# Low parts of the streamed weights of an attention stage, tied on VectorE to the scaling of the scores last written

## The chip, the cores and the metric

The kernel runs on one core of a Trainium2 chip. The metric is the time of one execution on the device in microseconds. Three timed runs of the kernel before the change took 1510.47 to 1513.23 us, with a median of 1512.52 us. One execution more was recorded by the profiler.

## The reference

One encoder layer works on 512 tokens of width 1024. One projection gives all inputs of two attentions of eight heads each: a neighbourhood attention in two dimensions and a latent attention with low-rank queries and keys. Their outputs, side by side, go through one output projection, a residual sum and a LayerNorm, and then through a layer of experts that is most of the time of the kernel and that this change does not touch.

```python
z = h @ W_in        # NA q | NA k | NA v | MLA c_q | MLA c_kv | MLA k_rope
a_na  = neighbourhood attention (8 heads, window 8 x 16, 2-D relative bias)
a_mla = latent attention (8 heads, low-rank q / kv, rotary key)
h = LN1(alpha * h + concat(a_na, a_mla) @ W_o)
h = LN2(alpha * h + PEER(h) + sigmoid(h @ W_g + b_g) * (p @ W_ple))
```

## The kernel before, in words

All products of weights and activations are made from split operands. `split` (L101 to L112) makes of a float32 tile a high part by a cast on ScalarE, and a low part, the difference of the tile and its high part, by a subtraction on VectorE. `mm3` (L122 to L125) then makes three matmuls: high by high, low by high, high by low. A weight is loaded by `stream` (L114): it takes one of three buffers `raw`, issues a DMA from SyncE, and splits into `whi` and `wlo`, of which there are two each. A buffer `raw` is free for the next load when both parts have been made of it.

The attention works in units, one for each head (or pair's half) and block of 128 query rows. Units 0 to 31 are those of the neighbourhood attention, in the first half of the stage, units 32 to 63 those of the latent attention. A unit has four steps: three matmuls give scores in PSUM; VectorE takes the maximum (L607 for the neighbourhood heads together with the bias, L718 for the latent ones) and negates it (L209), ScalarE takes the exponential with the sum (L210), VectorE the reciprocal (L211) and the scaling (L212), all but the maximum in `soft`; TensorE transposes the scaled scores (L219) and ScalarE copies them out (L221); TensorE multiplies them with the values (L622, L732). `run_heads` emits the scores of a unit two units ahead of its transposes, and in between the steps of the next heads' projections (`feeds`).

`next_weight` (L487) hands a projection its weight and at once prefetches the following one, so a weight has one projection's time to arrive and be split. The order of its users on TensorE is query, key and so on, as in `srcs`. `load_w2` (L737 to L742) loads the second half of the output weight w_o in four quarters and splits them into `w2h` and `w2l`, in one step of a feed; they are read only at the end of the output projection.

What sets the order: on TensorE the order is the one in which the code is written (`manual_schedule` with that engine alone). On VectorE, ScalarE, SyncE and GpSimd a scheduler of the framework orders the instructions, by its own model of costs, under the dependencies that it knows. A caller can add a dependency that orders two instructions on an engine without a semaphore: `split` does it for every entry of the list `turned`, which holds one instruction for the cast and one for the subtraction. In the stage of the change the list is empty before.

Of the kernel before, what the change touches and what calls it, by code (L numbers as in the profile page):

```python
# [15 lines left out]
OP = mybir.AluOpType  # L16
# [57 lines left out]
def tile_encoder_layer(ctx: ExitStack, tc: tile.TileContext, A: dict, out: bass.AP):  # L74
    nc = tc.nc
# [20 lines left out]
    def r32(ap):  # L96
        return ap.bitcast(F32)

    turned = []

    def split(hi, lo, src, scale=None):  # L101

        if scale is None:
            cut = nc.scalar.copy(hi, src), nc.vector.tensor_tensor(lo, src, r32(hi), op=OP.subtract)  # L104
            for ins, prev in zip(cut, turned):
                tc.add_manual_dep(ins.ins, prev.ins.name, mybir.DependencyInfo(mybir.DependencyClass.NoSync,
                                                                               mybir.DependencyReason.DATA),
                                  reason="order")
            return cut
        else:  # L110
            nc.scalar.mul(hi, src, scale)
            nc.vector.scalar_tensor_tensor(lo, src, scale, r32(hi), op0=OP.mult, op1=OP.subtract)  # L112

    def stream(src, shape, scale=None):  # L114
        raw = wst.tile([128] + shape, F32, name="raw", bufs=3)
        nc.sync.dma_start(raw, src)
        hi = wst.tile([128] + shape, F32R, name="whi")
        lo = wst.tile([128] + shape, F32R, name="wlo")
        cut = split(hi, lo, raw, scale)
        return (hi, lo, cut[0]) if cut else (hi, lo)  # L120
# [73 lines left out]
    def transpose_to(dst_h, dst_l, src, c):  # L194

        for g in range(2):
            ps = ps_tile("tr")
            for i in range(4):
                d = 4 * g + i
                nc.tensor.transpose(ps[:, i * 128:(i + 1) * 128], src[:, d * 128:(d + 1) * 128], ident)  # L200
            v = ps.rearrange("p (a b) -> p a b", b=128)
            cut = split(dst_h[:, 4 * g:4 * g + 4, c * 128:(c + 1) * 128],
                        dst_l[:, 4 * g:4 * g + 4, c * 128:(c + 1) * 128], v)
        return cut

    def soft(s_in, p, nk, mx, scale=1.0, minus=-1.0):

        mx, nmx, sm, rs = (mx[:, i:i + 1] for i in range(4))
        nc.vector.tensor_scalar(nmx, mx, minus, None, op0=OP.mult)  # L209
        nc.scalar.activation(p[:, :nk], s_in, AF.Exp, bias=nmx, scale=scale, accum_out=sm)  # L210
        nc.vector.reciprocal(rs, sm)  # L211
        nc.vector.tensor_scalar(p[:, :nk], p[:, :nk], rs, None, op0=OP.mult)  # L212

    def transposed(p, nk):
        ps = ps_tile("tr")
# [62 lines left out]
    with tc.tile_pool(name="ln0", bufs=1, reuse_waits="tile") as ln0, \  # L278
# [126 lines left out]
        for x in parts:  # L405
            split(*x)
# [80 lines left out]
    def next_weight():  # L487
        w = ready.pop() if ready else stream(*srcs.pop(0))
        if srcs:
            ready.append(stream(*srcs.pop(0)))  # L490
        return w

    def latent_k(i, lat):
# [44 lines left out]
    def latent_q(i):  # L538
        w = next_weight()
        ps = ps_tile("pj")  # L540
        yield from proj_steps(ps, w)
        split(cqh[:, i], cql[:, i], ps, gq[:, i:i + 1])
        if i == 0:
            nc.scalar.activation(sq_q, ps, AF.Square)
        else:
            sq = aw.tile([128, T], F32, name="p_exp", bufs=4)
            nc.scalar.activation(sq, ps, AF.Square)
            nc.vector.tensor_tensor(sq_q, sq_q, sq, op=OP.add)
# [12 lines left out]
    def rope_key():  # L561
        w = next_weight()
        ps = ps_tile("pj")
        yield from proj_steps(ps[:64], w, 64)
        kt = aw.tile([128, T], F32, name="p_exp", bufs=4)[:32]
        kt2 = aw.tile([128, T], F32, name="p_exp", bufs=4)[:32]
        nc.vector.tensor_tensor(kt, ps[0:32], cosT[0:32], op=OP.mult)
        nc.vector.tensor_tensor(kt2, ps[32:64], sinT[32:64], op=OP.mult)
        nc.vector.tensor_tensor(kt, kt, kt2, op=OP.add)
        split(krh, krl, kt)  # L570
# [10 lines left out]
    def na_proj(m):  # L581
        w = next_weight()
        ps = ps_tile("pj")
        yield from proj_steps(ps, w)
        qh, ql = na_q[m % 2]
        for hh in range(2):
            rows = slice(64 * hh, 64 * hh + 64)
            split(qh[rows, hh], ql[rows, hh], ps[rows], 0.125)
        w = next_weight()
        ps = ps_tile("pj")  # L590
        yield from proj_steps(ps, w)
        kh = ip.tile([128, T], F32R, name="na_kh")
        kl = ip.tile([128, T], F32R, name="na_kl")
        split(kh, kl, ps)
        na_k[m] = (kh, kl)

    def na_scores(m, b, hh):
        (qh, ql), (kh, kl) = na_q[m % 2], na_k[m]
        bias = ip.tile([128, NA_KEYS], F32, name="na_b", bufs=4)
        nc.gpsimd.dma_start(bias, A["na_bias"][2 * m + hh, b])  # L600
        qs = slice(b * 128, (b + 1) * 128)
        ks = slice(NA_FROM[b], NA_FROM[b] + NA_KEYS)
        ps = ps_tile("mm")
        mm3(ps[:, :NA_KEYS], (qh[:, hh, qs], ql[:, hh, qs]), (kh[:, ks], kl[:, ks]), True, True)
        p = aw.tile([128, 512], F32, name="p_exp", bufs=4)
        mx = small.tile([128, 4], F32, name="mx")
        nc.vector.tensor_tensor_reduce(p[:, :NA_KEYS], ps[:, :NA_KEYS], bias, op0=OP.add, op1=OP.max,  # L607
                                       accum_out=mx[:, 0:1], scale=1.0, scalar=LOW)
        soft(p[:, :NA_KEYS], p, NA_KEYS, mx)
        return p  # L610
# [97 lines left out]
    def mla_scores(m, c, par):  # L708
        nonlocal n_sc
        b = m % 2  # L710
        qs = slice(c * 128, (c + 1) * 128)
        kk = slice(0, 128 if par else 96)
        (qh, ql), (kh, kl) = qpar[par, b], kpar[par, b]
        ps = psH.tile([128, 512], F32, name="hp") if n_sc % 3 == 2 and n_sc > 2 else ps_tile("mm")
        n_sc += 1
        mm3(ps, (qh[kk, qs], ql[kk, qs]), (kh[kk, :], kl[kk, :]), True, True)
        mx = small.tile([128, 4], F32, name="mx")
        nc.vector.reduce_max(mx[:, 0:1], ps, axis=AX.X)  # L718
        p = aw.tile([128, 512], F32, name="p_exp", bufs=4)
        soft(ps, p, 512, mx, rq[:, c:c + 1], nrq[:, c:c + 1])  # L720
        return p
# [15 lines left out]
    def load_w2():  # L737
        for kk in range(4):
            raw = wst.tile([128, 2, 512], F32, name="raw", bufs=3)
            nc.sync.dma_start(raw, A["w_o"][kk * 256:(kk + 1) * 256, 512:1024].rearrange("(k p) n -> p k n", p=128))  # L740
            split(late_tiles["w2h"][:, 2 * kk:2 * kk + 2], late_tiles["w2l"][:, 2 * kk:2 * kk + 2], raw)
        yield  # L742

    def na_done():
# [6 lines left out]
    for m in range(1, 4):  # L751
        feeds += [(m, na_proj(m)), (4, latent_q(m - 1))]
    feeds += [(4, latent_values()), (4, latent_q_scale())]
    feeds += [(4 + m, mla_proj(m)) for m in range(4)] + [(8, load_w2())]
    with tc.manual_schedule(engines={nc.tensor.engine}):
        lat_k = []
# [171 lines left out]
    rs = pR.enter_context(tc.tile_pool(name="rs", bufs=1, reuse_waits="tile"))  # L928
# [666 lines left out]
```

## Time and profile before

| | us |
|---|---|
| median of three timed runs | 1512.52 |
| lowest, highest | 1510.47, 1513.23 |
| the profiled execution, its own time | 1511.24 |
| its span from first to last instruction | 1509.1 |

In the span TensorE is busy 98%, VectorE 86%, ScalarE 43% and GpSimd 38%. Busy shares are means over stages with different limits, so the rows below are read by stretch: from about 76 to 262 us for the attention, of which 84 to 173 us hold the neighbourhood units and 170 to 257 us the latent ones; the output projection runs from 228 to 297 us. In a timeline row the first number is the start, the second the duration; what stands in brackets is how long the engine was idle before it and which instruction ended that.

### The profile page before, as it was taken

How to read it: one execution, taken by the hardware profiler on the slowest of the kernel's cores; microseconds unless marked ns; L12 is line 12 of the kernel's file. 1: busy time of each engine (PE TensorE's matmuls, PEld its weight loads, DVE VectorE, ACT ScalarE, POOL GpSimd, SP SyncE). 2: the span in 40 equal slices, each digit the busy share in tenths (PEclk: the TensorE clock that was granted, in tenths of full speed). 3: DMA queues.
4: the chain of work that ended last, by engine and by line, in shares of the span. 5: the costliest groups of instructions: out<-in, count | busy, mean ns of one | idle time of the engine just before them, and what ended most of it. 6: DMA issues, size and time to landing. Idle time of an engine off the chain costs nothing.

```text
span 1509.1 us, 23088 instructions
## 1 busy us (share of the span) xinstructions
PE 1482.4 (98%) x7757; PEld 1256.0 (83%) x7757; DVE 1304.7 (86%) x3020; ACT 656.4 (43%) x1224; POOL 567.2 (38%) x520
## 2 busy tenths in 40 slices
PE   9999999999999999999999999999999999999997
PEld 5788767788888889888888988898888888888885
DVE  7376786679989998899888979999989999999997
ACT  3355676333322566213766644444433333333343
POOL 1013110010014343355542336555545666666530
PEclk9999999999999999999999999999999999999998
DMA  7333340052269999999999999999999999999992
GB/s 251 98 114 97 85 126 29 28 157 85 73 210 335 355 398 379 416 404 403 400 415 369 390 381 413 417 414 416 409 405 378 411 411 410 412 412 412 412 375 84
DMA packets 194359, 459.89 MB, mean 305 GB/s; under 512 B 18241, under 2 KB 97985, under 8 KB 192706
## 3 DMA queue, kind: packets, MB, share of 16 engines
q1 hardware_dynamic: 121856, 214.60, 38.8%
q0 software_dynamic: 57984, 207.12, 35.0%
q10 hardware_dynamic: 14402, 36.71, 6.3%
q8 instruction: 61, 1.00, 0.2%
q14 instruction: 56, 0.46, 0.1%
HBM read 414.59 MB, written 40.89 MB: 302 GB/s over the span
## 4 chain that ended last, share of the span: by engine, by line
PE 75%; DVE 11%; DMA 6%; issue 3%; ACT 2%; POOL 1%; SPq 0%; DVEq 0%; POOLq 0%; ACTq 0%
PE acc L1420 34%; PE mm L1186 5%; PE hp L1186 5%; PE tr L1044 4%; PE mm L123 3%; PE mm L124 3%; PE mm L125 3%; PE pj L123 3%; PE pj L124 3%; PE pj L125 3%; DMA whi<-in_u_rows_dram,s_ix 2%; DMA wlo<-in_u_rows_dram,s_ix 2%; PE hp L123 2%; PE hp L125 2%; PE hp L124 2%
## 5 line engine op out<-in xcount | busy, mean ns | idle before, releaser
L1403 POOL DMA_INDIRECT gat<-in_v_rows_dram,i_sel x128 | 205.6, 1606 | 122.5 <-DVE base L1405 92.4
L1186 PE MATMUL mm<-whole,raw 128*128 128x256 f32 x848 | 190.9, 379 | 0.0
L1388 POOL DMA_INDIRECT gat<-in_u_rows_dram,i_sel x102 | 137.3, 1346 | 117.7 <-DVE hdot L1394 75.6
L1186 PEld LDWEIGHTS mm<-whole,raw 128*128 128x128 f32 x848 | 158.8, 190 | 20.3
L104 ACT CAST a_hi<-gt 128x384 fp32r<-128x384 f32 x126 | 64.7, 514 | 251.7 <-PE acc L1420 132.8
L104 DVE TENSOR_TENSOR wlo<-raw,whi 128x1024 fp32r<-128x1024 f32 (+4 forms) x117 | 136.4, 1166 | 40.0 <-ACT whi L104 38.7
L1405 DVE SCALAR_TENSOR_TENSOR base<-gat,hdot,base 128x1024 f32<-128x1024 f32 x128 | 164.1, 1282 | 1.7
L104 ACT CAST whi<-raw 128x1024 fp32r<-128x1024 f32 (+4 forms) x117 | 117.2, 1003 | 96.7 <-PE mm L124 41.2
L1420 PE MATMUL acc<-v_hi,a_hi 128*128 128x512 f32 x480 | 148.8, 390 | 0.0
L1420 PE MATMUL acc<-v_lo,a_hi 128*128 128x512 f32 x480 | 148.5, 389 | 0.0
L1420 PE MATMUL acc<-v_hi,a_lo 128*128 128x512 f32 x480 | 148.4, 389 | 0.0
L1099 POOL DMA_INDIRECT whi<-in_u_rows_dram,s_ix x51 | 56.0, 1097 | 203.0 <-DVE cand L947 133.6
L1394 DVE CUSTOM_DVE_ANT_0 scr<-gat,h 128x1024 f32<-128x1024 f32 x102 | 124.7, 1223 | 2.1
L104 ACT CAST v_hi<-v_raw 128x1024 fp32r<-128x1024 f32 x80 | 84.0, 1050 | 77.5 <-issue 31.7
L1082 DVE TENSOR_SCALAR oh_j<-iota,eT 128x128 f32<-128x128 f32 x384 | 113.5, 370 | 0.0
L1420 PEld LDWEIGHTS acc<-v_lo,a_hi 128*128 128x128 f32 x480 | 90.1, 188 | 19.0
L1420 PEld LDWEIGHTS acc<-v_hi,a_lo 128*128 128x128 f32 x480 | 90.1, 188 | 18.9
L104 DVE TENSOR_TENSOR v_lo<-v_raw,v_hi 128x1024 fp32r<-128x1024 f32 x80 | 97.7, 1221 | 7.6 <-ACT v_hi L104 7.6
L1420 PEld LDWEIGHTS acc<-v_hi,a_hi 128*128 128x128 f32 x480 | 88.2, 188 | 16.9 <-ACT a_hi L104 0.3
L1044 PEld LDWEIGHTS tr<-oh_i,oh_j 128*128 128x128 f32 x768 | 93.3, 192 | 9.4 <-ACT g_st L1056 5.5
L1044 PE MATMUL tr<-oh_i,oh_j 128*128 128x128 f32 x768 | 95.5, 276 | 4.1 <-DVE oh_j L1082 2.5
L1099 POOL DMA_INDIRECT wlo<-in_u_rows_dram,s_ix x51 | 62.3, 1221 | 83.9 <-DVE s_dot L1101 45.4
(391 smaller groups left out, 3500.4 us busy)
## 6 DMA issues: line engine op xcount, KB each, us to landing
raw<-in_uT_dram SPq DMA_DIRECT2D x103, 512.0 KB, 7.5
v_raw<-in_v_rows_dram SPq DMA_DIRECT2D x82, 512.0 KB, 12.7
g_dram<-g_st ACTq DMA_DIRECT2D x12, 2048.0 KB, 10.8
gt<-g_dram SPq DMA_DIRECT2D x60, 384.0 KB, 13.5
raw<-in_v_rows_dram SPq DMA_DIRECT2D x44, 512.0 KB, 12.9
raw_u<-in_uT_dram SPq DMA_DIRECT2D x25, 512.0 KB, 6.9
ge_dram<-ge ACTq DMA_DIRECT2D x88, 128.0 KB, 6.6
ge<-ge_dram SPq DMA_DIRECT2D x88, 128.0 KB, 12.3
```

Source lines behind the costliest of these rows:

```text
L104: cut = nc.scalar.copy(hi, src), nc.vector.tensor_tensor(lo, src, r32(hi), op=OP.subtract)
L123: nc.tensor.matmul(ps, a[0], b[0], start=start, stop=False)
L124: nc.tensor.matmul(ps, a[0], b[1], start=False, stop=False)
L125: nc.tensor.matmul(ps, a[1], b[0], start=False, stop=stop)
L1044: nc.tensor.matmul(ps[:, i * 128:(i + 1) * 128], oj[:, 4 * r + i, :], oi[:, 4 * r + i, :], start=True, stop=True)
L1099: nc.gpsimd.indirect_dma_start(out=u[:], out_offset=None, in_=u_rows, in_offset=bass.IndirectOffsetOnAxis(ap=ix[:, k:k + 1], axis=0))
L1186: nc.tensor.matmul(ps[:, :N_U], raw[:, k], whole[:, k, :], start=(k == 0), stop=(k == 7))
L1388: nc.gpsimd.indirect_dma_start(out=u[:], out_offset=None, in_=u_rows, in_offset=bass.IndirectOffsetOnAxis(ap=i_sel[:, c, k:k + 1], axis=0))
L1394: nc.vector.tensor_tensor_reduce(scr, u, h[c], op0=OP.mult, op1=OP.add, accum_out=hdot[:, c, k:k + 1], scale=1.0, scalar=0.0)
L1403: nc.gpsimd.indirect_dma_start(out=u[:], out_offset=None, in_=v_rows, in_offset=bass.IndirectOffsetOnAxis(ap=i_sel[:, c, k:k + 1], axis=0))
L1405: nc.vector.scalar_tensor_tensor(base[c], u, hdot[:, c, k:k + 1], base[c], op0=OP.mult, op1=OP.add)
L1420: nc.tensor.matmul(acc[c][hf], a[:, cs], b[:, hf * 512:(hf + 1) * 512], start=(n == 0 and i == 0), stop=(n == 127 and i == 2))
```

## The change

`soft` keeps its scaling in a list `scaled`, in the place of a subtraction (the place of a cast holds nothing). `next_weight`, where it prefetches, and `load_w2` put that entry into `turned` while they split, so that VectorE may make the low part only after the scaling last written in the code. `split` skips the place that holds nothing: the cast on ScalarE is free as before. Nothing is added to or taken from the work, and no wait between engines is added by the dependency itself, since both ends are on VectorE.

```diff
--- before.py
+++ after.py
@@ -103,6 +103,8 @@
         if scale is None:
             cut = nc.scalar.copy(hi, src), nc.vector.tensor_tensor(lo, src, r32(hi), op=OP.subtract)
             for ins, prev in zip(cut, turned):
+                if prev is None:
+                    continue
                 tc.add_manual_dep(ins.ins, prev.ins.name, mybir.DependencyInfo(mybir.DependencyClass.NoSync,
                                                                                mybir.DependencyReason.DATA),
                                   reason="order")
@@ -203,13 +205,15 @@
                         dst_l[:, 4 * g:4 * g + 4, c * 128:(c + 1) * 128], v)
         return cut
 
+    scaled = []
+
     def soft(s_in, p, nk, mx, scale=1.0, minus=-1.0):
 
         mx, nmx, sm, rs = (mx[:, i:i + 1] for i in range(4))
         nc.vector.tensor_scalar(nmx, mx, minus, None, op0=OP.mult)
         nc.scalar.activation(p[:, :nk], s_in, AF.Exp, bias=nmx, scale=scale, accum_out=sm)
         nc.vector.reciprocal(rs, sm)
-        nc.vector.tensor_scalar(p[:, :nk], p[:, :nk], rs, None, op0=OP.mult)
+        scaled[:] = [None, nc.vector.tensor_scalar(p[:, :nk], p[:, :nk], rs, None, op0=OP.mult)]
 
     def transposed(p, nk):
         ps = ps_tile("tr")
@@ -487,7 +491,9 @@
     def next_weight():
         w = ready.pop() if ready else stream(*srcs.pop(0))
         if srcs:
+            turned.extend(scaled)
             ready.append(stream(*srcs.pop(0)))
+            turned.clear()
         return w
 
     def latent_k(i, lat):
@@ -738,7 +744,9 @@
         for kk in range(4):
             raw = wst.tile([128, 2, 512], F32, name="raw", bufs=3)
             nc.sync.dma_start(raw, A["w_o"][kk * 256:(kk + 1) * 256, 512:1024].rearrange("(k p) n -> p k n", p=128))
+            turned.extend(scaled)
             split(late_tiles["w2h"][:, 2 * kk:2 * kk + 2], late_tiles["w2l"][:, 2 * kk:2 * kk + 2], raw)
+            turned.clear()
         yield
 
     def na_done():
```

The scheduler then comes to other orders on VectorE, ScalarE and GpSimd in the attention, from about 76 to 262 us; SyncE's order stays; TensorE's changes in its last part only, where thirteen matmuls of the output projection (L123 to L125 with `aTh`) no longer stand between the scores of unit 53 and the transposes of unit 52 but later, most of them behind the transposes of unit 58. The lines of the kernel after are numbered higher by 2 from L106 on, by 4 from L206 on, by 6 from L492 and by 8 from L742 on.

The first place is on VectorE, before the scaling of unit 29 (p_exp_1606 is unit 29, p_exp_1642 unit 30; wlo_1616 is the low part of the key weight of the first latent pair). Before:

```order
L209 TENSOR_SCALAR mx_1585<-mx_1585 128x1
L672 TENSOR_TENSOR pj_1532<-pj_1532,sinT_105 128x512
L104 TENSOR_TENSOR wlo_1616<-raw_1613,whi_1615 128x256
L211 RECIPROCAL mx_1585<-mx_1585 128x1
L673 TENSOR_TENSOR p_exp_1594<-p_exp_1594,pj_1532 128x512
L212 TENSOR_SCALAR p_exp_1584<-p_exp_1584,mx_1585 128x256
L607 ISA p_exp_1606,mx_1607<-mm_1602,na_b_1600 128x256
```

After:

```order
L613 ISA p_exp_1642,mx_1643<-mm_1638,na_b_1636 128x256
L613 ISA mx_1643 128x1
L213 TENSOR_SCALAR mx_1607<-mx_1607 128x1
L104 TENSOR_TENSOR hTl_90<-pj_1619,hTh_89 64x512
L213 TENSOR_SCALAR mx_1643<-mx_1643 128x1
L215 RECIPROCAL mx_1607<-mx_1607 128x1
L216 TENSOR_SCALAR p_exp_1606<-p_exp_1606,mx_1607 128x256
L104 TENSOR_TENSOR wlo_1616<-raw_1613,whi_1615 128x256
L104 TENSOR_TENSOR hTl_90<-pj_1619,hTh_89 64x512
```

The low part stood between the rotary steps of the queries and now stands behind the scaling of unit 29.

The second place is on VectorE, around unit 47 (mx_2128 and p_exp_2130; wlo_2138 is the low part of a query weight of the last latent pair, hTl_90 that of a head's projection). Before:

```order
L209 TENSOR_SCALAR mx_2099<-mx_2099,nrq_440 128x1
L104 TENSOR_TENSOR wlo_2138<-raw_2135,whi_2137 128x384
L104 TENSOR_TENSOR hTl_90<-pj_2054,hTh_89 64x512
L211 RECIPROCAL mx_2099<-mx_2099 128x1
L718 TENSOR_REDUCE mx_2128<-mm_2124 128x1
L212 TENSOR_SCALAR p_exp_2101<-p_exp_2101,mx_2099 128x512
L209 TENSOR_SCALAR mx_2128<-mx_2128,nrq_440 128x1
L104 TENSOR_TENSOR hTl_90<-pj_2054,hTh_89 64x512
```

After:

```order
L724 TENSOR_REDUCE mx_2128<-mm_2124 128x1
L213 TENSOR_SCALAR mx_2128<-mx_2128,nrq_440 128x1
L104 TENSOR_TENSOR hTl_90<-pj_2054,hTh_89 64x512
L215 RECIPROCAL mx_2128<-mx_2128 128x1
L216 TENSOR_SCALAR p_exp_2130<-p_exp_2130,mx_2128 128x512
L104 TENSOR_TENSOR wlo_2138<-raw_2135,whi_2137 128x384
L104 TENSOR_TENSOR hTl_90<-pj_2141,hTh_89 64x512
L104 TENSOR_TENSOR wlo_2170<-raw_2167,whi_2169 128x256
L724 TENSOR_REDUCE mx_2181<-mm_2177 128x1
```

The low part moved behind the maximum, the negation and the scaling of unit 47.

The third place is on VectorE, the quarters of the output weight (w2l_1807). Before, the first of them stands ahead of the scaling of unit 42 (p_exp_1997), the others at three later places:

```order
L718 TENSOR_REDUCE mx_2023<-hp_2019 128x1
L211 RECIPROCAL mx_1995<-mx_1995 128x1
L104 TENSOR_TENSOR w2l_1807<-raw_2330,w2h_1806 128x1024
L104 TENSOR_TENSOR aTl_98<-p_exp_1978,aTh_97 128x512
L212 TENSOR_SCALAR p_exp_1997<-p_exp_1997,mx_1995 128x512
L104 TENSOR_TENSOR aTl_98<-hp_1855,aTh_97 128x512
```

After, three of them stand behind the scaling of unit 53 (p_exp_2325) and ahead of the reciprocal and scaling of unit 54 (p_exp_2359); the fourth comes further down, before the reciprocal of unit 55:

```order
L215 RECIPROCAL mx_2323<-mx_2323 128x1
L213 TENSOR_SCALAR mx_2357<-mx_2357,nrq_440 128x1
L216 TENSOR_SCALAR p_exp_2325<-p_exp_2325,mx_2323 128x512
L104 TENSOR_TENSOR w2l_1807<-raw_2330,w2h_1806 128x1024
L104 TENSOR_TENSOR w2l_1807<-raw_2334,w2h_1806 128x1024
L104 TENSOR_TENSOR w2l_1807<-raw_2338,w2h_1806 128x1024
L215 RECIPROCAL mx_2357<-mx_2357 128x1
L724 TENSOR_REDUCE mx_2383<-hp_2379 128x1
L216 TENSOR_SCALAR p_exp_2359<-p_exp_2359,mx_2357 128x512
```

Three subtractions moved from separate places, two of them around units 42 and 44, to one place eleven units later.

## Rows read from the trace of the kernel before

**Rows 1.** The page, section 4: shares of the chain that ended last, by engine
```profile
PE 75%; DVE 11%; DMA 6%; issue 3%; ACT 2%; POOL 1%; SPq 0%; DVEq 0%; POOLq 0%; ACTq 0%
```

**Rows 2.** Stretches: us, then busy PE, PEld, DVE, ACT, POOL; clock; DMA share; GB/s
```profile
180.00:184.00 4.00, 4.00 (x26) 3.18 (x24) 2.16 (x7) 2.14 (x5) 0.00 (x0) 0.57 0.11 34
200.00:220.00 20.00, 17.50 (x117) 12.93 (x116) 17.34 (x37) 15.08 (x30) 3.91 (x8) 1.00 0.55 158
```

**Rows 3.** TensorE timeline: start, us, line, names, shapes; in brackets idle before it
```profile
83.03 0.39 PE L125 MATMUL pj<-hTh,wlo 128*128 128x512 f32 x1
...
163.86 0.39 PE L125 MATMUL pj<-ckh,wlo 128*128 128x512 f32 x1
...
167.65 0.47 PE L123 MATMUL pj<-cqh,whi 128*128 128x512 f32 x1 [1.15 <-DVE hTl L104]
...
179.56 0.50 PE L123 MATMUL mm<-hTh 96*128 96x512 f32 x1 [1.45 <-ACT p_exp L210]
...
202.52 0.30 PE L219 MATMUL tr<-ident,p_exp 128*128 128x128 f32 x1 [1.57 <-DVE p_exp L212]
...
213.26 0.40 PE L125 MATMUL pj<-cqh,wlo 128*128 128x512 f32 x1
...
214.54 0.50 PE L124 MATMUL mm<-hTl,hTh 96*128 96x512 f32 x1 [0.48 <-DVE hTl L104]
...
221.91 0.30 PE L219 MATMUL tr<-ident,p_exp 128*128 128x128 f32 x1 [0.38 <-DVE p_exp L212]
...
232.88 1.09 PE L732 MATMUL hp<-p_t,v_mla 128*64 128x128 f32 x16
...
235.84 0.38 PE L219 MATMUL tr<-ident,p_exp 128*128 128x128 f32 x2
```

**Rows 4.** VectorE timeline, the same columns
```profile
82.21 0.27 DVE L209 TENSOR_SCALAR mx<-mx 128x1 f32<-128x1 f32 x2
...
160.88 0.41 DVE L104 TENSOR_TENSOR wlo<-raw,whi 128x256 fp32r<-128x256 f32 x1
...
163.03 0.43 DVE L607 CUSTOM_DVE_ANT_0 p_exp<-mm,na_b 128x256 f32<-128x256 f32 x1 [0.81 <-PE tr L219]
...
201.90 0.48 DVE L212 TENSOR_SCALAR p_exp<-p_exp,mx 128x512 f32<-128x512 f32 x1
...
206.08 0.48 DVE L212 TENSOR_SCALAR p_exp<-p_exp,mx 128x512 f32<-128x512 f32 x1
...
213.28 0.49 DVE L212 TENSOR_SCALAR p_exp<-p_exp,mx 128x512 f32<-128x512 f32 x1
...
233.56 0.48 DVE L212 TENSOR_SCALAR p_exp<-p_exp,mx 128x512 f32<-128x512 f32 x1
```

**Rows 5.** VectorE groups, 84 to 262 us: count, busy, mean ns, idle before
```profile
L718 DVE TENSOR_REDUCE mx<-mm 128x1 f32<-128x512 f32 x23 | 15.7, 687 | 2.2 <-PE mm L125 1.9
...
L104 DVE TENSOR_TENSOR hTl<-pj,hTh 64x512 fp32r<-64x512 f32 x16 | 10.9, 684 | 0.4 <-ACT hTh L104 0.2
L211 DVE RECIPROCAL mx<-mx 128x1 f32<-128x1 f32 x64 | 10.2, 160 | 19.5 <-ACT p_exp L210 18.8
...
L104 DVE TENSOR_TENSOR w2l<-raw,w2h 128x1024 fp32r<-128x1024 f32 x4 | 4.9, 1225 | 0.7 <-ACT w2h L104 0.6
...
L104 DVE TENSOR_TENSOR wlo<-raw,whi 128x384 fp32r<-128x384 f32 x4 | 2.2, 548 | 0.0
```

**Rows 6.** ScalarE groups, 84 to 262 us, the same columns
```profile
L221 ACT COPY p_t<-tr 128x512 f32<-128x512 f32 x48 | 28.1, 585 | 18.5 <-PE tr L219 18.1
...
L104 ACT CAST hTh<-pj 64x512 fp32r<-64x512 f32 x16 | 9.1, 579 | 0.3
...
L104 ACT CAST w2h<-raw 128x1024 fp32r<-128x1024 f32 x4 | 4.2, 1050 | 1.2 <-DMA raw<-in_w_o_dram 1.1
```

**Rows 7.** ScalarE timeline, the exponential of unit 47
```profile
212.18 0.79 ACT L210 ACTIVATE p_exp<-mm,mx,rq 128x512 f32<-128x512 f32 x1
```

**Rows 8.** The loads of L740: DMA issue to landing
```profile
DMA to landing us min/median/max: 3.7/4.1/4.5
```

## The prediction

> **What bounds the kernel now.** I read the chain of waits first. The reader is to see that 75% of the chain that ended last is TensorE and only 11% VectorE [rows 1]: a VectorE instruction costs time only where TensorE stands still for it. So I went to the one stage whose order changes, the attention between about 76 and 262 us, and asked the view by stretches where TensorE has gaps. From 200 to 220 us TensorE is busy 17.50 of 20.00 us and VectorE 17.34 [rows 2]: there the two run nearly level, and what stands ahead of a scaling on VectorE is seen by the transposes. Last I read TensorE's own timeline for the places that matter: those at which it waits in the run before, and those at which it first reads a low part that has been moved [rows 3]. At the first kind it idled 1.15 us at 167.65, 1.45 at 179.56, 1.57 at 202.52, 0.48 at 214.54 and 0.38 at 221.91. That is the pool from which a gain must come, some 5 us. From the end of the stage on the orders of all engines are as before, so what is lost or won in the stage reaches the end of the span in full.
>
> **What the edit does to the order.** Nineteen low parts of next weights and the four of w2 are now tied to a scaling on VectorE; none is added or dropped, so the work is conserved. TensorE's own stream only has thirteen matmuls of the output projection moved, from before unit 55 to after unit 58, and SyncE's stream is the same. So the sum is a sum of waits, at five places.
>
> **A, the first prefetched weight (wlo_672), +0.7.** TensorE reads it at 83.03 without waiting [rows 3]. In the new order it stands after the maxima and negations of units 0 to 2 and the scaling of unit 0. In the run before those negations ended at 82.21 + 0.27 = 82.48 [rows 4]; with a reciprocal of 0.16 [rows 5], a scaling of at most 0.49 [rows 4] and a low part of 1024 columns, 1.22 [rows 5], it would be there at 84.35, 1.3 late. But the old low part stood ahead of these maxima; with all of its 1.22 given back it is there at 83.13, 0.1 late. I take the middle, because the scores of unit 2 do not come sooner. The other low parts of the neighbourhood heads are behind the scaling of a unit whose successor weight is first read a whole pair of units later; I cost them at nothing. Their cover is the projection in progress; without it each would cost up to its 1.22.
>
> **B, the key weight of the first latent pair (wlo_1616), +1.0.** Now done at 160.88 + 0.41, read at 163.86 [rows 3, 4]. It moves behind the scaling of unit 29. That unit's maximum starts at 163.03 only, when a transpose frees its buffer [rows 4], and now the maximum of unit 30 and one low part of a head (0.684 [rows 5]) stand between. From 163.03: two maxima of 0.43 each, with the reading of their results half a microsecond, that low part, the reciprocal (0.16), a scaling (at most 0.49), then 0.41, ends near 166.0; with the waits between engines I take 2.2 after the reader. Then the old one at 167.65 (1.15 [rows 3]) falls away, because the buffer it waited for is free by then: 2.2 - 1.15, about 1.0. Bounds: 0, if the new wait is as short as the old; 2.2, if the old one stays.
>
> **C, unit 42, -0.8.** Its transposes idle 1.57 at 202.52 for a scaling that starts at 201.90 [rows 3, 4], behind a 1.22 us quarter of w2 (w2l_1807 of raw_2330 in the order shown). That quarter leaves. A low part of a head output comes ahead in its place (the nearest row is 0.684 [rows 5]), partly beside the exponential. Bounds -1.2 and -0.5; I take -0.8, since the cast of that output now also precedes the exponential on ScalarE.
>
> **D, the query weight of the last pair (wlo_2138), +1.6.** It now follows the scaling of unit 47, which before ended at 213.28 + 0.49 = 213.77 [rows 4]. That scaling itself becomes later. The first quarter of w_o can be loaded only when wlo_2051 has released its buffer, and wlo_2051 now stands behind the scaling of unit 44 (206.08 + 0.48 [rows 4], then 0.41 as for wlo_1616): issue near 207.0, landing 4.1 later [rows 8], at 211.1, cast until 212.1 (1.05 [rows 6]). ScalarE does this cast, then a high part (0.58) and a copy (0.59) [rows 6] ahead of the exponential of unit 47, so that starts at 213.3. It started at 212.18 before [rows 7], so everything behind it is 1.1 later: scaling done at 214.9, low part (0.55 [rows 5]) at 215.4, TensorE's read at 213.26 [rows 3] late by 2.2. The low part of the key head queued behind it (0.684) is there at 216.1, where the scores of unit 48 needed it at 214.54 [rows 3]: +1.6. The old waits there are inside this difference. Bounds: 0.5, if the exponential is not late, and 2.0, with a landing of 4.5.
>
> [...]
>
> **E, the second half of w_o, +4.6.** Three quarters' low parts, each 1.225 [rows 5], now stand in a row behind the scaling of unit 53, ahead of the reciprocal and scaling of unit 54 and, ahead of that scaling, the maximum of unit 55. In the run before the scaling of unit 54 ended at 233.56 + 0.48 = 234.04 and its transposes began at 235.84 [rows 3, 4], 1.80 to spare. Three times 1.225 and 0.687 for the maximum [rows 5] are 4.36; less 1.80 that is 2.6, the least it can cost with the old cover. But part of that cover was the output projection's matmuls, which are now behind unit 58; with no cover it would cost all of the 4.4. I take 3.3, a little nearer to the row. What is late next is the fourth quarter: its buffer is free when the first of the three is done, 2.45 before the last ends; landing 4.1 after that [rows 8] is 1.65 behind the third; cast 1.05, which ScalarE now does ahead of the exponential of unit 55, 2.7; from the start of an exponential to that of its scaling 1.10 (212.18 to 213.28 [rows 4, 7]), and the maximum of unit 57 now stands between, 0.69: 4.5; the scaling 0.49, 5.0. TensorE meanwhile has the transposes of unit 54, which may start 1.4 behind the third low part, then 1.09 for the values [rows 3] and the scores of unit 57, done near 3.5. So 1.5 more, 1.1 to 1.9 by the landings. I take 1.7, since each step between engines adds a little. Against these stands 0.4: the 0.38 at 221.91 [rows 3] goes, with three long low parts gone from ahead of unit 48. Together 3.3 + 1.7 - 0.4 = 4.6, bounds 3.3 and 5.9.
>
> **The sum.** 0.7 + 1.0 - 0.8 + 1.6 + 4.6 = 7.1. The profiled execution took 1511.24 us (span 1509.1, 2.1 around it), so 1518.3. That execution is 1.28 below the median of the three timed runs, 1512.52, which spread from 1510.47 to 1513.23; the forecast is 0.47% above the one and 0.38% above the other. Measurement of this kernel tells about 0.2%, 3.0 us, from no change.
>
> **Rivals.**
>
> [...]
>
> Cover holds, no change, 1512.6. Maximum and scaling of later units could make up A, B and D, as every low part of a next weight has a projection's time; then E with its old cover (2.6) and the gains (-0.8, -0.4) remain: 1.4. For it: none of the waits of the run before ends with the low part of a weight [rows 3], so these had time to spare. Against: B and D rest on readers that come before the scaling.
>
> Scalings freed, faster, 1507.8. The place is the chain maximum, exponential, scaling, transposes of the latent units. If each scaling with no low part ahead is on time, the waits at 202.52, 221.91 and 179.56 (1.57, 0.38, 1.45) and the slow 4 us after the last (1.7) go: -5.1; with A and B left (+1.7) that is -3.4. It decides the time if VectorE is ahead of TensorE by more than the 3.7 us of three quarters when it comes to unit 53. Against: with 17.34 of 20 us busy it is hardly ahead anywhere, and the run before had 1.80 to spare there.
>
> **How the numbers follow.** Forecast 0.48, its own range 1515.6 to 1520.5; clock 0.20; cover 0.20; freed 0.12. Slower by over 0.2% are the first two, 0.68; within 0.2% the third, 0.20; faster the last, 0.12. The range of 8 in 10 leaves out most of the freed case and the far tail of the clock case with all upper bounds: 1510.5 to 1521.8.
>
> **What would show it.** TensorE with an idle of 2 us or more before the first matmul that reads wlo_1616 and before the transposes of unit 54, the latter released by the scaling; VectorE with three low parts of w2 one behind the other just ahead of it; the exponential of unit 55 held by the cast of the fourth quarter. Wrong would be a transpose of unit 54 that starts on time, a clock of 1.00 with no waits near 180 us, or an out projection that starts earlier than 228 us.

## The result and the profile after

| | before | after |
|---|---|---|
| median of six timed runs, us | 1513.2 | 1524.46 |
| lowest, highest | 1510.47, 1515.55 | 1522.91, 1527.9 |
| the profiled execution, its own time | 1511.24 | 1523.64 |
| its span | 1509.1 | 1521.7 |

The change makes the kernel slower: ratio 1.0076, interval 1.0063 to 1.009. The forecast was 1518.3 with a range up to 1521.8. The direction was right, and the time lies above the range. By medians the change costs 11.3 us, between the two profiled executions 12.4. I start with the places that the prediction named. TensorE's timeline of the kernel after (start, us, names, in brackets the idle before it and what ended it):

```profile
83.98 0.50 PE L127 MATMUL pj<-hTh,wlo 128*128 128x512 f32 x1 [0.47 <-DVE wlo L104]
...
167.47 0.50 PE L127 MATMUL pj<-ckh,wlo 128*128 128x512 f32 x1 [1.73 <-DVE wlo L104]
...
184.01 0.50 PE L125 MATMUL mm<-hTh 96*128 96x512 f32 x1 [1.45 <-ACT p_exp L214]
...
204.54 0.63 PE L223 MATMUL tr<-ident,p_exp 128*128 128x128 f32 x4 [0.72 <-DVE mx L213]
...
216.75 0.76 PE L125 MATMUL pj<-cqh,whi 128*128 128x512 f32 x1 [2.97 <-DVE hTl L104]
...
218.50 0.80 PE L127 MATMUL pj<-cqh,wlo 128*128 128x512 f32 x1 [0.56 <-DVE wlo L104]
...
243.16 0.63 PE L223 MATMUL tr<-ident,p_exp 128*128 128x128 f32 x4 [2.02 <-DVE mx L213]
...
248.36 0.63 PE L223 MATMUL tr<-ident,p_exp 128*128 128x128 f32 x4 [1.27 <-DVE mx L215]
```

The first two rows and the one at 218.50 wait for the low part of a weight, at the readers of A, B and D; before, none did [rows 3]. The old 1.15 at 167.65 is gone, the 1.57 at 202.52 is 0.72, the 0.38 at 221.91 is gone. The rows at 243.16 and 248.36 are the transposes of units 54 and 55. What VectorE does ahead of them:

```profile
238.47 3.49 DVE L104 TENSOR_TENSOR w2l<-raw,w2h 128x1024 fp32r<-128x1024 f32 x3
241.88 0.15 DVE L215 RECIPROCAL mx<-mx 128x1 f32<-128x1 f32 x1
241.95 0.67 DVE L724 TENSOR_REDUCE mx<-hp 128x1 f32<-128x512 f32 x1
242.54 0.48 DVE L216 TENSOR_SCALAR p_exp<-p_exp,mx 128x512 f32<-128x512 f32 x1
```

and ScalarE ahead of the exponential of unit 55:

```profile
214.23 1.04 ACT L104 CAST w2h<-raw 128x1024 fp32r<-128x1024 f32 x1 [2.41 <-DMA raw<-in_w_o_dram]
...
243.57 1.04 ACT L104 CAST w2h<-raw 128x1024 fp32r<-128x1024 f32 x1 [2.46 <-DMA raw<-in_w_o_dram]
244.53 0.77 ACT L214 ACTIVATE p_exp<-hp,mx,rq 128x512 f32<-128x512 f32 x1
```

Three low parts stand in a row, then reciprocal, maximum and scaling. The wait at 243.16 is put down to a negation, but the scaling ended at 242.54 + 0.48 = 243.02, just ahead of the transposes. The cast of the fourth quarter (243.57) waits for its load and holds the exponential. This is the mechanism of E as forecast, but not its sizes. The two stalls forecast for units 54 and 55, 3.3 and 1.7, are waits of 2.02 and 1.27, and three waits that were not on the list stand ahead of them, at the values of an earlier unit and at the transposes of units 51 and 52:

```profile
232.89 1.09 PE L738 MATMUL hp<-p_t,v_mla 128*64 128x128 f32 x16 [0.57 <-DVE mx L213]
...
235.65 0.63 PE L223 MATMUL tr<-ident,p_exp 128*128 128x128 f32 x4 [0.78 <-DVE mx L213]
...
237.46 0.63 PE L223 MATMUL tr<-ident,p_exp 128*128 128x128 f32 x4 [0.48 <-DVE p_exp L216]
```

In the kernel before, the thirteen matmuls of the output projection stood just ahead of these two transposes, seven and six, of which the last are shown; the change takes them away:

```profile
229.52 0.39 PE L123 MATMUL pj<-whi,aTh 128*128 128x512 f32 x1
229.75 0.60 PE L219 MATMUL tr<-ident,p_exp 128*128 128x128 f32 x4
...
232.04 0.39 PE L123 MATMUL pj<-whi,aTh 128*128 128x512 f32 x1
232.32 0.63 PE L219 MATMUL tr<-ident,p_exp 128*128 128x128 f32 x4
```

So a part of E came at the places that lost their cover, ahead of unit 54. The cast at 214.23 is the one of D.

What was not forecast at this size is in the view by stretches (us, busy PE, PEld, DVE, ACT, POOL, granted clock, DMA share, GB/s), after:

```profile
168.00:172.00 4.00, 4.00 (x25) 3.06 (x25) 2.40 (x8) 1.56 (x3) 0.43 (x1) 0.61 0.73 198
...
180.00:184.00 4.00, 1.59 (x7) 0.91 (x7) 3.85 (x9) 2.91 (x7) 0.00 (x0) 1.00 0.82 205
...
216.00:224.00 8.00, 6.69 (x29) 4.72 (x29) 4.34 (x9) 3.80 (x9) 0.00 (x0) 0.57 0.40 131
244.00:248.00 4.00, 3.09 (x19) 1.94 (x15) 2.18 (x4) 3.57 (x7) 0.00 (x0) 0.58 0.66 220
```

Three stretches have a granted clock of 0.57 to 0.61, where before there was one, 0.57 at 180 to 184 [rows 2]; the full slices of 1 us inside them (169 to 172, 217 to 223, 244 to 247) read 0.50. In slices of 1 us, one minus the granted clock sums to 1.71 us lost before and 6.83 after: one step of 1.7 against four. At 180 to 184, the place of before's fall, the clock now stays at 1.00.

For all kernels below I use the same two numbers of the profiled execution: the stage, from TensorE's first scores to the first transposes of the norm (75.00 to 284.81 before), and what the clock lost in it by that sum. The difference of the two holds the work and the waits; since a part of a fall can lie in an idle (at 218 to 219 after, TensorE was busy 0.50 of 1.00 us at a clock of 0.50), it can be an estimated few tenths too low.

| kernel | ratio to before, interval | stage, us | clock lost | difference |
|---|---|---|---|---|
| before | | 209.81 | 1.71 | 208.10 |
| before, second profile (e8) | 1.0001 [0.9991, 1.0012] | 210.10 | 1.70 | 208.40 |
| after | 1.0076 [1.0063, 1.009] | 222.83 | 6.83 | 216.00 |
| after, second profile (e7) | 1.0085 [1.0072, 1.0099] | 221.36 | 5.12 | 216.24 |
| e1, weights alone tied | 1.0045 [1.0033, 1.0057] | 217.11 | 5.11 | 212.00 |
| e2, w2 alone tied | 1.0042 [1.0028, 1.0057] | 216.27 | 3.41 | 212.86 |
| e3, wlo_2051 free | 1.0065 [1.0047, 1.0083] | 222.61 | 8.52 | 214.09 |
| e4, key product twice | 1.0067 [1.0052, 1.0083] | 219.21 | 1.70 | 217.51 |
| e5, w2 loaded late | 1.001 [0.9998, 1.0021] | 208.87 | 0 | 208.87 |
| e6, three fills | 1.0084 [1.0065, 1.0102] | 221.50 | 5.12 | 216.38 |

So the stage is 13.0 longer after: 7.9 in waits, where the sum was 7.1, and 5.1 in the clock, where the sum had nothing. Between the second executions of the two kernels it is 11.3: 7.8 in waits and 3.4 in the clock. My theory after the result: the sum of the five terms is nearly right, and the rest is the clock. The rivals: a wait that I mis-sized (the 2.97 of D above all), and falls that belong to certain waits, so that each wait has its price.

### The profile page after: what moved, and what is told of

It is laid out like the page before. It is cut to its first block, busy times and chain, and to the rows that moved or that the text cites. A ratio compares the mean times of both kernels' runs of the same rounds, so it can differ in the third digit from the quotient of the medians.

```text
span 1521.7 us, 23080 instructions
## 1 busy us (share of the span) xinstructions
PE 1486.3 (98%) x7757; PEld 1257.5 (83%) x7757; DVE 1308.0 (86%) x3020; ACT 655.4 (43%) x1224; POOL 570.2 (37%) x520
## 4 chain that ended last, share of the span: by engine, by line
PE 83%; DVE 11%; DMA 3%; ACT 2%; issue 1%; POOL 0%; SPq 0%; DVEq 0%; ACTq 0%; POOLq 0%
PE acc L1428 34%; PE mm L1194 13%; PE hp L1194 5%; PE tr L1052 4%; PE mm L125 3%; PE mm L126 3%; PE mm L127 3%; PE pj L125 3%; PE pj L127 3%; PE pj L126 3%; PE hp L125 2%; PE hp L127 2%; PE hp L126 2%; PE tr L223 1%; PE tr L896 1%
```

## Experiments

**e1 and e2: each half of the change alone.** e1 takes the two lines on `turned` out of `load_w2`, e2 those out of `next_weight`:

```diff
-            turned.extend(scaled)
             split(late_tiles["w2h"][:, 2 * kk:2 * kk + 2], late_tiles["w2l"][:, 2 * kk:2 * kk + 2], raw)
-            turned.clear()
```

> The tie of the w_o quarters is undone, that of the next weights stays. By my account of the changed trace (TensorE's delay against before: 2.2 from the two ties of wlo_672 and wlo_1616, -0.8 at unit 42, 4.7 around units 47 to 50, 5.9 from unit 48 to 57) the last part goes and the rest stays, since wlo_2051 is still behind the scaling of unit 44 and the load of the first quarter behind it: 6 to 7.5 above before, about 1520. If the quarters cost nothing where they stand in the changed kernel: no better than it, 1524.

> Only the w_o quarters are tied, the low parts of the next weights are free as before. My account: the delays at wlo_672, wlo_1616 and around unit 47 go, the gain at unit 42 stays (-0.8, and -0.4 at unit 47), four low parts in a row behind the scaling of unit 54 cost 4 to 6: 1516.5 to 1518. If instead it is the next weights alone that cost: 1512 to 1513, as before or better.

Medians 1518.88 and 1519.43, 6.9 and 7.5 above the 1511.94 of before in that series. The waits of e1, and then those of e2:

```profile
167.32 0.50 PE L127 MATMUL pj<-ckh,wlo 128*128 128x512 f32 x1 [1.74 <-DVE wlo L104]
...
217.38 0.77 PE L125 MATMUL pj<-cqh,whi 128*128 128x512 f32 x1 [3.77 <-DVE hTl L104]
```

```profile
167.83 0.47 PE L125 MATMUL pj<-cqh,whi 128*128 128x512 f32 x1 [1.15 <-DVE hTl L104]
...
179.73 0.79 PE L125 MATMUL mm<-hTh 96*128 96x512 f32 x1 [1.45 <-ACT p_exp L214]
...
202.15 0.41 PE L223 MATMUL tr<-ident,p_exp 128*128 128x128 f32 x2 [1.17 <-DVE p_exp L216]
...
237.70 0.45 PE L223 MATMUL tr<-ident,p_exp 128*128 128x128 f32 x1 [4.54 <-DVE mx L215]
```

A, B and D come from the weights, E from w2: without the weights' ties the old 1.15 stands as before and the waits of the low parts are gone. C does not need the tie of the quarters. In e1 they are free, and still unit 42 waits 0.73 as in after:

```profile
204.35 0.63 PE L223 MATMUL tr<-ident,p_exp 128*128 128x128 f32 x4 [0.73 <-DVE mx L213]
```

The first quarter's load there waits for the buffer of wlo_2051, which is tied, and its low part comes at 215.16 only. With w2 alone tied (e2) the wait is 1.17, so that half gives 0.4 of the 0.8. By the last column of the table e1 costs 3.9 (A to D were 2.5 on record) and e2 4.8 (E was 4.6). Together that is 8.7 where both halves at once cost 7.9; why they do not add up was not tried. The clock takes 3.4 more than before in e1 and 1.7 more in e2. e1 came out inside its expectation, e2 above it.

**e3: the load of D comes in time.** `if len(srcs) != 3:` ahead of `turned.extend(scaled)` in `next_weight` leaves wlo_2051 alone untied.

> The changed kernel, with one tie less: the low part wlo_2051, whose buffer the first w_o quarter takes, is free. wlo_2138 is still behind the scaling of unit 47. If the loss around unit 47 (4.7) comes by way of the late load (buffer, transfer, ScalarE's cast ahead of the head's high part, then the clock): 3 to 4 us come back, 1520.5 to 1521.5. If it comes from wlo_2138 standing behind that scaling: under 1 us comes back, 1523.5 to 1524.5.

The 2.97 is gone; what remains at this place is the low part itself, and unit 42 waits longer (1.25) than after:

```profile
205.82 0.41 PE L223 MATMUL tr<-ident,p_exp 128*128 128x128 f32 x2 [1.25 <-DVE p_exp L216]
...
217.20 0.50 PE L127 MATMUL pj<-cqh,wlo 128*128 128x512 f32 x1 [1.59 <-DVE wlo L104]
```

The waits are 1.9 shorter, so D's chain through the buffer of wlo_2051 is shown by the trace. The time does not show it: the median is 1523.8 (1524.46 after), in the range that was expected of the other cause, the intervals of the two ratios overlap, the six runs spread from 1518.7 to 1526.77, and the profiled one, the slowest of them, lost 8.52 to the clock. The rival of a single mis-sized wait falls by size: without the longest wait 1.9 come back, and 5.1 were missing.

**e4 and e6: work in the place of idle.** e4 adds the lines with the plus to the key product of the last latent pair, so that it is done twice on the same values (6 matmuls). e6 has these, six single matmuls ahead of the first read of wlo_1616, and the scores of unit 56 three times.

```diff
             mm3(psk, (w[0][:, k], w[1][:, k]), (ckh[:, k, :], ckl[:, k, :]), k == 0, k == 1)
+            if m == 2 and k == 1:
+                for k in range(2):
+                    mm3(psk, (w[0][:, k], w[1][:, k]), (ckh[:, k, :], ckl[:, k, :]), k == 0, k == 1)
```

> The changed kernel, with the six matmuls of one key projection (pj of wlo_2051, just ahead of TensorE's longest idle, 2.97 us) done twice: 1.4 us more work for TensorE with the same values. If the granted clock falls there because TensorE stood idle, and the fall costs 1.5 or more, the longer activity keeps it: 1523 or below, 1 to 1.5 us faster than the changed kernel although it does more. If the clock falls anyway: no change, 1524 to 1525. If the repeated work delays the head's high part: 1525.5.

> The kernel after, with work repeated on TensorE ahead of three of its waits, on the same values, so that only the time changes: six single matmuls ahead of the first read of wlo_1616, the key projection of the last latent pair a second time, and the scores of unit 56 three times over; some 18 matmuls, about 4 us of work, most of it inside waits. VectorE, ScalarE and the loads keep their orders. If the missing part of the prediction is the granted clock (three falls more than before, 1.7 us each, after waits of 1.7 to 3 us), shorter waits leave at most one or two falls, and the time is 1517 to 1521, that is 3 to 7 below the kernel after although it does more. If the waits themselves are the missing part and the clock only follows, the repeated work is hidden at best: 1523 to 1526. If falls come from elsewhere, they stay at four and the time is 1524 to 1528.

e4: median 1520.85, with more work on TensorE than after; by the intervals of the ratios e4 is not told from after. Its profile has after's waits of B and E, but one fall only:

```profile
167.08 0.50 PE L127 MATMUL pj<-ckh,wlo 128*128 128x512 f32 x1 [1.73 <-DVE wlo L104]
...
238.96 0.45 PE L223 MATMUL tr<-ident,p_exp 128*128 128x128 f32 x1 [2.02 <-DVE mx L213]
```

```profile
167.00:173.00 6.00, 5.92 (x40) 4.75 (x41) 5.29 (x15) 3.15 (x9) 1.03 (x3) 1.00 0.55 147
180.00:188.00 8.00, 6.55 (x45) 5.19 (x46) 6.09 (x17) 4.45 (x11) 0.00 (x0) 1.00 0.42 136
239.00:243.00 4.00, 4.00 (x23) 2.91 (x23) 2.05 (x4) 3.54 (x7) 0.00 (x0) 0.58 0.78 252
```

The fall is gone at D, where the work was added, but also at B, where nothing was changed, so the added work is not shown to be what kept the clock. Nor was it hidden: the last column is 1.3 to 1.5 above after's, about the 1.4 us of the six matmuls (an estimate from three of this product in after, which start at 211.80, 212.04 and 212.26, 0.23 apart).

e6: median 1523.74, no better than after, against the 1517 to 1521 expected if shorter waits leave one or two falls. The wait at wlo_1616 shrank from 1.73 to 0.38 and the one at unit 54 from 2.02 to 0.67, and no fall came at these two. But two steps in a row came behind the 1.45, which was not filled, and a third, at 219 to 222 us, behind a wait of 1.05 at D:

```profile
166.79 0.50 PE L127 MATMUL pj<-ckh,wlo 128*128 128x512 f32 x1 [0.38 <-DVE wlo L104]
...
181.74 0.80 PE L125 MATMUL mm<-hTh 96*128 96x512 f32 x1 [1.45 <-ACT p_exp L214]
```

```profile
181.00:189.00 8.00, 7.26 (x32) 5.66 (x33) 4.21 (x13) 3.01 (x7) 0.00 (x0) 0.57 0.31 112
```

The repeated work, an estimated 4 us (18 matmuls at 0.23), is hidden (216.38 against 216.00 to 216.24). Filling three of the waits left three steps, as many as the second execution of after has, so the time did not come down, and a fixed price for each wait is not borne out. The ratios of e4 and e6 have overlapping intervals; that e4 is the faster is not shown.

**e7 and e8: both kernels again, unchanged.**

> The kernel after, unchanged, with a second profile. The first profile lost 6.8 us of full clock in four steps of 1.7 us: one at 168 to 173, two at 216 to 224, one at 244 to 248. If a fall belongs to a place (a wait of some length at it), the second profile has the same falls at the same places, within 1 us, and the same waits. If a fall is a matter of the execution, the waits ended by low parts are the same within 0.2 us (0.47 at 84, 1.73 at 167, the two between 216 and 219, the two between 243 and 249), but the falls stand elsewhere or are fewer or more, by multiples of 1.7. In both cases the median is 1522 to 1527, 11 to 14 above the run before of the same series.

> The kernel before, unchanged, with a second profile. The first lost 1.7 us in one step, at 180 to 184, behind its wait of 1.45. If a fall belongs to that wait, it is there again; if it is a matter of the execution, there are 0 to 2 falls at other places, and the waits are the same within 0.2 us. Median 1510 to 1514. Mean of the granted clocks over the runs 0.996 to 0.998, where the kernel after has 0.993 to 0.995: 3 to 6 us of the difference of the two kernels.

After, second profile, waits and falls:

```profile
167.33 0.50 PE L127 MATMUL pj<-ckh,wlo 128*128 128x512 f32 x1 [1.74 <-DVE wlo L104]
...
182.30 0.50 PE L125 MATMUL mm<-hTh 96*128 96x512 f32 x1 [1.45 <-ACT p_exp L214]
...
215.49 0.47 PE L125 MATMUL pj<-cqh,whi 128*128 128x512 f32 x1 [1.83 <-DVE hTl L104]
...
217.24 0.50 PE L127 MATMUL pj<-cqh,wlo 128*128 128x512 f32 x1 [1.05 <-DVE wlo L104]
...
241.32 0.30 PE L223 MATMUL tr<-ident,p_exp 128*128 128x128 f32 x1 [2.02 <-DVE mx L213]
```

```profile
168.00:172.00 4.00, 4.00 (x33) 3.12 (x32) 3.40 (x11) 2.69 (x6) 0.27 (x1) 1.00 0.66 194
...
183.00:187.00 4.00, 4.00 (x26) 2.95 (x24) 2.46 (x8) 1.96 (x5) 0.00 (x0) 0.57 0.05 20
217.00:221.00 4.00, 3.76 (x11) 2.66 (x11) 2.80 (x6) 0.58 (x1) 0.00 (x0) 0.58 0.54 171
241.00:245.00 4.00, 3.68 (x22) 2.94 (x23) 2.40 (x6) 3.23 (x7) 0.00 (x0) 0.57 0.82 251
```

The 1.73 at 167 is there again and this time no fall follows; the 1.45, behind which the first profile had none, now has one. Only the two waits of D differ by more than 0.2: 1.83 for 2.97 and 1.05 for 0.56. The load behind it was issued at 208.48 and its cast began at 212.97, against 208.60 and 214.23 in the first profile. Before, second profile, has its fall at 180 to 184 again, but e5, with the same 1.45 at 179.56, stays at 1.00 there:

```profile
180.00:184.00 4.00, 4.00 (x32) 3.19 (x31) 3.02 (x10) 2.23 (x5) 0.00 (x0) 1.00 0.11 33
```

So behind a wait of this length a fall is a matter of the execution: one may follow. For the longer ones the record says more. The ten profiles of the table have 44 waits of TensorE of 1 us or more in the stage, and every fall in it began within such a wait or at most 1.7 us after one. Each fall is put down to the last wait begun; two of the shorter waits, the 1.27 of after and of e3, came while the clock was low already:

| waits in the stage, ten profiles | number | with a fall | steps of 1.7 us |
|---|---|---|---|
| 1.0 to 1.9 us | 37 | 11 | 13 |
| 2.0 us and more (2.02, 2.97, 3.77, 4.54) | 7 | 7 | 10 |

The 1.45 is in all ten and has a fall in six. The 2.02 ahead of unit 54 is in four and has one in all four, in both executions of after too. Since four of the seven long waits are this one, it is not shown whether their length or their place counts.

Over all runs with a clock on record, the mean granted clock is 0.9967 for before (26 runs of the last series) and 0.9936 for after (11 runs); 0.0031 of 1520 us is an estimated 4.7 us, near the 5.1 and 3.4 of the profiles, so the profiled executions were not odd ones.

**e5: the loop of `load_w2` behind the first half's matmuls**, no ties; the quarters then stand in the trace behind the scalings of units 52, 56, 60 and 63 (counted from 0; the expectation counts them from 1).

> The kernel before, without any tie, and with the loop that loads the second half of w_o written behind the first half's matmuls instead of in the latent stage: its quarters then come on VectorE behind the scalings of units 53, 57, 61 and 64, each alone, instead of 42, 45, 48 and 48. Same work. If the quarters cost time because they stand ahead of scalings where VectorE is level with TensorE (units 42 to 55), the waits of the run before at 202.52 (1.57) and 221.91 (0.38) go and nothing takes their place: 1.5 to 2.5 below the run before of the same series. If the quarters are only moved to other scalings that are as short of time, no change within 0.2%. If the matmuls of the second half now wait for the last quarter, 1 to 4 slower. On the granted clock: one fall of 1.7 us near 180 as before, none elsewhere, if falls follow the added waits.

Median 1513.48 against 1511.28; the interval of the ratio includes 1, so no difference is shown. The 1.57 at 202.52 shrinks to 0.73, but a wait of the old length comes at unit 50:

```profile
224.03 0.41 PE L219 MATMUL tr<-ident,p_exp 128*128 128x128 f32 x2 [1.57 <-DVE p_exp L212]
```

The quarters were not what unit 42's wait hung on alone. Nor are falls confined to the stage: this profile has none in it but one at 778 us, among the experts (0.59, 0.50, 0.50 and 0.70 in the slices from 778 to 782, 1.71 us lost). None of the variants beats before.

## Why the prediction was wrong

The terms, by how far TensorE's rows of the two kernels move apart between one place and the next, less the clock of the stretch (first profile; e7 gives the same sum to 0.3):

| term | on record | measured |
|---|---|---|
| A | +0.7 | +0.7, and 0.3 more near 146 us that was not listed |
| B | +1.0 | +1.5 |
| C | -0.8 | -0.8 |
| D | +1.6 | +1.3 |
| E, both stalls and the three waits ahead of them | +5.0 | +5.5 |
| E, the 0.38 at 221.91 | -0.4 | -0.5 |
| sum (the rounded terms measured give 8.0) | 7.1 | 7.9 |

The step that failed is in "How the numbers follow": the clock case had 0.20, and it was one fall, 1.7 us (4.00 us at 0.57 [rows 2]), at E alone, 1520.0. The kernel after had three steps more than before in its first profile and two more in its second. What the runs showed in its place is 3.4 to 5.1 us of clock beyond before, behind several of the new waits. Of the three waits over 1 us before, the 1.45 has a fall (0.57 at 180 to 184 [rows 2]) and the 1.57 and the 1.15 have none (1.00 at 200 to 220 [rows 2] and at 167 to 171); the forecast took no fall at all for four new waits (B, D, and two in E). One fall in two waits, by the 1.45 and the 1.57, would have given two falls, 3.4 us, and a forecast of 1521.7; one in three, with the 1.15 as well, 2.3 us and 1520.6. Neither is all of it: the forecast itself had waits of 2.2 us at B and 3.3 at E, longer than any of before, so no row of before could price them. In the ten profiles all waits of that length cost at least one step. The sum of the waits, by contrast, was close, in part by luck: E came near its size with the waits at other places than forecast.

The traces show the falls of the stage behind waits of 1 us or more (none began later than 1.7 us after one), and the same wait in the same kernel with and without a fall (1.73 us at 167 with, 1.74 without).

The smaller steps: in D the load was issued at 208.60 where 207.0 was on record, mostly the 2.0 by which the stage was late by then; its cast began 5.6 behind the issue, 4.5 in the second execution, where 4.1 was taken. That D still came out 0.3 below its term is in part luck. The loads of w2 after, answering to [rows 8]:

```profile
DMA to landing us min/median/max: 3.9/4.5/5.1
```

Why this load was 1.1 slower in one execution than in the other wasn't tried. In B the reader waited 1.73 where 2.2 was taken, but a second wait of 0.5 arose at 162 ahead of it. Of the tests named in advance, the three low parts, the late scaling of unit 54, the cast ahead of the exponential of unit 55 and the out projection (first matmul at 253 us instead of 228) came as forecast; the wait at wlo_1616, 1.73, stayed below the 2 us named.

The rivals "cover holds" and "scalings freed" are out: the tied weights of A, B and D made their readers wait, and the 1.45 that "scalings freed" needed gone is still there.

## What to carry to other kernels

A low part pushed behind a scaling on VectorE came back here as the wait of its own reader on TensorE (0.47 us at A, 1.73 at B, 0.56 at D), and three pushed to one point, 3.49 us of work, made one long wait (2.02 at unit 54); size each by its reader's slack in the trace. Take the clock into the sum as an expected value, not as a mishap to one side: number the new waits by length, and ask for each length how many such waits in the traces at hand show a fall. Here waits of 2 us and more had one in 7 of 7 cases, shorter ones in 11 of 37; where the trace of before has no wait as long as a forecast one, its price is unknown and the range has to hold it. And compare two executions before a place is blamed: most waits of after repeated to 0.01 us (1.73 and 1.74, 1.45 twice, 2.02 twice, 1.27 twice), the falls behind the shorter ones did not (one and none behind the 1.73, none and one behind the 1.45).

## What the runs showed of the hardware

Falls of the granted clock came in steps that cost 1.7 us each (4 us at 0.57), one, two in a row, or none behind the same wait of 1.45 us; behind the seven waits of 2 us and more there was always one. The same kernel's executions differ by some 4 us and more, in part for that reason: in e4's six runs, those at a mean clock of 0.996 to 0.997 took 1519.63 to 1520.96, those at 0.993 to 0.994 took 1524.59 and 1525.18. But the clock does not explain all of it: in e6 three runs at 0.996 took 1521.7, 1524.69 and 1526.25, and one at 0.991 took 1524.96. What decides whether a given shorter wait is followed by a fall stays open; filling waits with work did not settle it.
